# SBUF start addresses of matmul operands in a hybrid attention and convolution layer: pools in another order, small constants in one filled-up tile

## The chip, the cores and the metric

The kernel runs on one core of a Trainium2 chip. The metric is the device time of one execution in microseconds; the time before is the median of three executions.

## What is computed

One layer over 1024 positions of 1024 features, all in float32. The reference, cut to what matters:

```python
h = rms_norm(x, pre_norm_gain)
q, k, v, z_a, b_gate, c_gate, u, z_c = jnp.split(h @ w_in, 8, axis=-1)
attn = diff_attention(q, k, v, lam, slopes)        # 4 heads, two softmax maps each, chunk-causal
attn = rms_norm(attn, subln_gain, 1e-5) * 0.8 * silu(z_a)
conv_out = b_gate * conv3(c_gate * u) * silu(z_c)
mixed = jnp.concatenate([attn, conv_out], axis=-1) @ w_out
x = x + rms_norm(mixed, post_norm_gain)
e = rms_norm(p @ w_ple_proj, ple_norm_gain)
out = x + jax.nn.sigmoid(x @ w_ple_gate) * e
```

## The kernel before

Features lie on the 128 partitions, positions along the free dimension; the 1024 positions are two halves of 512 columns, and 1024 features are eight tiles of 128 (`kt`). Every float32 product is made of three matmuls in the 4-byte float32r type: `split` (L81 to L87) writes a value as a high and a low part, and `mm3` (L93 to L96) issues high x high (L94), high x low (L95) and low x high (L96) into one PSUM bank. The first operand, `lhsT`, is the stationary one, 128 columns loaded before each matmul; the second, `rhs`, streams through, 512 columns as a rule.

The stages, in order of time:

- the layer embedding (`embed`, tile `ple`), which starts while the inputs still arrive;
- the input projections (`product`, L122 to L126, tile `pj`): weight tiles `w` are stationary, the normalised input `hT` streams; each product of one weight tile with one half is 24 matmuls;
- the values (`v`): here slices of `hT` are stationary and the weights `wv` stream;
- per head, scores (L232, tile `s`, `qs` stationary, `ks` streaming), softmax, transposes of the probabilities (L259, tile `tpw`), and the product with the values (tile `av`, `vs` stationary, `wt` streaming), with the convolution's projections (`pj` again) laid between them by the table `PLAN`;
- the output projection (`out_half`, tile `o<-mT`), its norm (`post`, L529 to L537), and the gate (`gate_half`, L541 to L559, tile `o<-x`), which for each tile and half loads `e` from DRAM (L546), scales it (L547), waits for the product's tanh (L556), finishes `e` (L557, L558) and stores it (L559). `e` has three buffers.

The tiles `mT` and `x` of the last stage use the buffers of `hT`. The order of instructions on each engine comes from a scheduler that simulates the program; transfers all go through the SyncE queue.

SBUF space is given out in the order in which pools are opened and tiles are taken from them, each tile at the next multiple of 32 bytes. Before, pool `const` comes first (L49) and holds, beside two 512-byte matrices, five tiles of 16 to 148 bytes; everything after it starts at an odd multiple of 32. Start addresses, in bytes modulo 512, of what the matmuls read:

| matmuls | streaming operand | starts at | stationary operand | starts at | count |
|---|---|---|---|---|---|
| `pj`, `o` | hT, mT, x | 32 | w | 192 | 2136 |
| `v` | wv | 288 | hT | 32 | 192 |
| `ple`, `s`, `av` | pth, ks, wt | 288 | wph, qs, vs | 288 | 432 |
| `tpw` | ident | 128 | p0 to p3 | 288 | 144 |

Of the kernel before, what the change touches and what calls it, by code (L numbers as in the profile page):

```python
# [12 lines left out]
F32 = mybir.dt.float32  # L13
# [7 lines left out]
P = 128  # L21
S = 1024
D = 1024
NT = S // P
KT = D // P
HALF = 512
# [17 lines left out]
def hybrid_layer(ctx, tc, xT, pT, w_in, small, lams, w_out, w_ple, w_gate, outT):  # L44
    nc = tc.nc
    V, A, T, G = nc.vector, nc.scalar, nc.tensor, nc.gpsimd
    mult, add, sub = ALU.mult, ALU.add, ALU.subtract

    const = ctx.enter_context(tc.tile_pool(name="const", bufs=1))  # L49
    dram = ctx.enter_context(tc.tile_pool(name="dram", bufs=1, space=DRAM))  # L50
    hp = ctx.enter_context(tc.tile_pool(name="hp", bufs=16))
    mixp = ctx.enter_context(tc.tile_pool(name="mixp", bufs=1))
    tiny = ctx.enter_context(tc.tile_pool(name="tiny", bufs=3))
    rawp = ctx.enter_context(tc.tile_pool(name="rawp", bufs=3))
    wp = ctx.enter_context(tc.tile_pool(name="wp", bufs=3))
    ps_s = ctx.enter_context(tc.tile_pool(name="ps_s", bufs=3, space=PSUM))
    ps_a = ctx.enter_context(tc.tile_pool(name="ps_a", bufs=1, space=PSUM))

    def bank_s(name):
        return ps_s.tile([P, HALF], F32, tag="s", bufs=3, name=name)  # L60
# [7 lines left out]
    ident = const.tile([P, P], F32, name="ident")  # L68
    make_identity(nc, ident)
    fold = const.tile([P, P], F32, name="fold")  # L70
    own = const.tile([P, 4], F32, name="own")
    nhalf = const.tile([P, 16], F32, name="nhalf")
    G.memset(nhalf, -0.5)
    sm = const.tile([P, 37], F32, name="sm")
    subg = const.tile([P, 1], F32, name="subg")
    rs_e = const.tile([P, 32], F32, name="rs_e")

    def col(base, k):
        return sm[:, base + k:base + k + 1]
# [9 lines left out]
    def rsqrt(out, ssq, n, eps):  # L89
        V.tensor_scalar(out=out, in0=ssq, scalar1=1.0 / n, scalar2=eps, op0=mult, op1=add)  # L90
        G.tensor_tensor(out=out, in0=out, in1=nhalf[:, :ssq.shape[-1]], op=ALU.pow)
# [7 lines left out]
    def column_sums(acc, pool, extra=None, tag="flip"):  # L99
        flip = pool.tile([P, HALF], F32, tag=tag, name="flip")  # L100
        V.transpose(out=flip, in_=acc)
        part = tiny.tile([P, 32], F32, tag="part", name="part")
        V.tensor_reduce(out=part[:, 0:16], in_=flip.rearrange("p (f r) -> p f r", r=32), axis=AX.X, op=add)
        if extra is not None:
            V.tensor_tensor(out=part[:, 16:32].rearrange("p (t f) -> p t f", t=4),
                            in0=extra.unsqueeze(2).broadcast_to([P, 4, 4]),
                            in1=own.unsqueeze(1).broadcast_to([P, 4, 4]), op=mult)
        n = 16 if extra is None else 32
        ms = bank_t("ms")
        T.matmul(out=ms[:, :n], lhsT=fold, rhs=part[:, :n], start=True, stop=True)  # L110
        return ms
# [30 lines left out]

    hT = operand("hT")
    mix = [[mixp.tile([P, HALF], F32, tag="mix", bufs=16, name=f"mix{k}_{n}") for n in range(2)] for k in range(KT)]
    gt = mixp.tile([P, HALF + 2], F32, name="gt")
    R = [const.tile([P, HALF], F32, name=f"R{n}") for n in range(2)]

    with ExitStack() as st:
        qk = st.enter_context(tc.tile_pool(name="qk", bufs=1))
        rowp = st.enter_context(tc.tile_pool(name="rowp", bufs=3))  # L150

        lam_in = gt[:, 0:256].rearrange("p (a b) -> p a b", a=4)
        lam_e = qk.tile([P, 2], F32, name="lam_e")
        nlam = qk.tile([P, 1], F32, name="nlam")

        def mixing_weight():
            nc.sync.dma_start(out=lam_in.rearrange("p a b -> p (a b)"), in_=lams.partition_broadcast(P))
# [11 lines left out]
        class Head:  # L169
# [45 lines left out]
            def softmax(s, i):  # L215
                ii = i % 4
                W = (i + 1) * P
                qi = slice(i * P, i * P + P)
                nm = tiny.tile([P, 4], F32, tag="nm", name="nm")
                l = tiny.tile([P, 2], F32, tag="l", name="l")  # L220
                first = min(W, HALF) if W - HALF >= 256 or W <= HALF else W - 256
                chunks = [(0, first), (first, W - first)][:1 if W <= HALF else 2]
                low = [3.0e38] * 2
                pr = [ap.tile([P, S], F32, tag=f"p{ii}", name=f"p{ii}"), a2.tile([P, S], F32, tag="p1", name="p1")]
                for ci, (c0, n) in enumerate(chunks):
                    nn = max(256, n)
                    c = slice(c0, c0 + nn)
                    b0 = S - W + c0
                    banks = [bank_s(f"s{m}") for m in range(2)]
                    for m in range(2):  # L230
                        for part in range(2):
                            T.matmul(out=banks[m][:, :nn], lhsT=s.qs[:, m, qi], rhs=s.ks[:, m, part, c],  # L232
                                     start=part == 0, stop=part == 1)
                    for m in range(2):
                        new = nm[:, 2 * m + ci:2 * m + ci + 1]
                        V.tensor_tensor_reduce(out=pr[m][:, c0:c0 + n], in0=banks[m][:, :n], in1=s.bias[:, b0:b0 + n],  # L236
                                               scale=-1.0, scalar=low[m], op0=add, op1=ALU.min, accum_out=new)
                        low[m] = new
                for m in range(2):
                    A.activation(out=pr[m][:, :W], in_=pr[m][:, :W], func=AF.Exp, scale=-1.0, bias=low[m],  # L240
                                 accum_out=l[:, m:m + 1])
                if ii == 0:
                    s.r0 = tiny.tile([P, 4], F32, tag="r0", name="r0")
                rl = tiny.tile([P, 1], F32, tag="rl", name="rl")
                V.reciprocal(out=s.r0[:, ii:ii + 1], in_=l[:, 0:1])
                V.reciprocal(out=rl, in_=l[:, 1:2])
                V.scalar_tensor_tensor(out=rl, in0=rl, scalar=l[:, 0:1], in1=nlam, op0=mult, op1=mult)
                V.scalar_tensor_tensor(out=pr[0][:, :W], in0=pr[1][:, :W], scalar=rl, in1=pr[0][:, :W], op0=mult, op1=add)
                s.ws[ii] = pr[0]
# [98 lines left out]
        with ExitStack() as st0:  # L348
            vp = st0.enter_context(tc.tile_pool(name="vp", bufs=1, reuse_waits="tile"))
            v2 = st0.enter_context(tc.tile_pool(name="v2", bufs=2, reuse_waits="tile"))  # L350
            r_col = qk.tile([P, NT], F32, name="r_col")

            def sums_x(n):
                acc = R[n]
                A.activation(out=acc, in_=mix[0][n], func=AF.Square)
                for kt in range(1, KT):
                    sq = rowp.tile([P, HALF], F32, tag="t", name="sqx")
                    A.activation(out=sq, in_=mix[kt][n], func=AF.Square)
                    V.tensor_tensor(out=acc, in0=acc, in1=sq, op=add)
                return acc  # L360

            def row_scale(n):
                r = tiny.tile([P, 16], F32, tag="rs", name="rsx")
                rsqrt(r, column_sums(sums_x(n), rowp, tag="t")[:, :16], D, 1e-6)
                spread(R[n], r)
                for g in range(4):
                    A.copy(out=r_col[32 * g:32 * g + 32, 4 * n:4 * n + 4], in_=r[32 * g:32 * g + 32, g:16:4])

            head0 = Head(0)
            row_scale(0)  # L370
            row_scale(1)
            run([(wq, head0.ev_q), (wk, head0.ev_k)], (0,))
            run([(wq, head0.ev_q), (wk, head0.ev_k)], (1,), bank_s)
            run([(w_in_tile(3, 0, V), head0.ev_z)])
            wv = vp.tile([P, 2, KT, HALF], F32R, name="wv")
            for h in range(H):
                raw = rawp.tile([P, KT, P], F32, tag="raw", name="raw")
                nc.sync.dma_start(out=raw, in_=w_in[8 + h])
                c = slice(h * P, (h + 1) * P)
                split(wv[:, 0, :, c], wv[:, 1, :, c], raw)  # L380
            for j in range(NT):
                c = slice(j % 4 * P, j % 4 * P + P)
                ps = bank_p("v")
                for kt in range(KT):
                    b = hT[j // 4][kt]
                    mm3(ps, b[:, 0, c], b[:, 1, c], wv[:, 0, kt], wv[:, 1, kt], kt == 0, kt == KT - 1)
                v = v2.tile([P, 2, HALF], F32R, tag="v", name="v")
                split(v[:, 0], v[:, 1], ps, r_col[:, j:j + 1])
                nc.sync.dma_start(out=v_dram[j], in_=v.bitcast(F32))
        ap = st.enter_context(tc.tile_pool(name="ap", bufs=1, reuse_waits="tile"))  # L390
        a2 = st.enter_context(tc.tile_pool(name="a2", bufs=2, reuse_waits="tile"))
# [224 lines left out]
```

## Time and profile before

| | before |
|---|---|
| median of 3 runs | 660.55 us (659.13 to 661.38) |
| the profiled execution: its own time | 659.43 us |
| the profiled execution: span, first to last instruction | 657.7 us |
| PE busy | 644.0 us (98%), 2941 matmuls |
| DVE busy | 447.0 us (68%) |
| ACT, POOL busy | 243.2 us (37%), 229.3 us (35%) |
| DMA, mean over the span | 67.77 MB, 103 GB/s |
| mean granted TensorE clock | 0.996 of full |

The duration that the profile gives to a matmul is modelled and holds the way through the array too, so that durations overlap. How fast matmuls follow each other is read from their start times.

### The profile page before, as it was taken

The page shows a single profiled execution, that of the slowest core. Times are in us where ns is not written, and L with a number is a line of the kernel's source. Part 1 is how long each engine was busy: PE and PEld are TensorE (multiplying, and loading weights), DVE is VectorE, ACT ScalarE, POOL GpSimd, SP SyncE. Part 2 cuts the span into 40 slices and gives each one's busy share as a digit, 9 for nine tenths or more (in the row PEclk, how much of TensorE's full clock was granted, in tenths as well). Part 3 has the DMA queues.
Part 4 walks back from the last instruction along what each step waited for, and adds up shares of the span by engine and source line. Part 5 has one row for each costly group of instructions (what it writes and reads, how often), then busy time and mean ns, then how long its engine had stood idle before and what let it go on. Part 6 is the DMA issues. An engine that isn't in the chain of part 4 may idle for free.

```text
span 657.7 us, 8063 instructions
## 1 busy us (share of the span) xinstructions
PE 644.0 (98%) x2941; PEld 523.8 (80%) x2941; DVE 447.0 (68%) x821; ACT 243.2 (37%) x442; POOL 229.3 (35%) x114
## 2 busy tenths in 40 slices
PE   8899999999999999999999999999999999999994
PEld 4688888888888888888888888888888888888884
DVE  6968412698686687876886999439781199796233
ACT  7944312333462333543344434113631227131110
POOL 2016100325236534256362142424560278460000
PEclk9999999999999999999999999999999999999998
DMA  8966522210254112352012400103240025142222
GB/s 283 402 252 192 191 97 89 90 47 3 78 145 134 43 33 80 103 156 64 33 48 81 129 32 33 64 33 129 69 155 0 22 75 192 33 144 97 95 81 96
DMA packets 35654, 67.77 MB, mean 103 GB/s; under 512 B 3744, under 2 KB 12448, under 8 KB 35616
## 3 DMA queue, kind: packets, MB, share of 16 engines
q1 hardware_dynamic: 35616, 67.27, 31.3%
q8 instruction: 23, 0.38, 0.2%
q14 instruction: 15, 0.12, 0.1%
HBM read 48.38 MB, written 12.58 MB: 93 GB/s over the span
## 4 chain that ended last, share of the span: by engine, by line
PE 83%; DMA 8%; DVE 6%; issue 1%; ACT 1%; SPq 0%; DVEq 0%
PE pj L96 16%; PE pj L95 16%; PE pj L94 16%; PE s L232 5%; PE o L95 5%; PE o L96 5%; PE o L94 5%; DMA e<-e_dram 4%; DMA out_dram<-e 3%; PE tpw L259 2%; PE v L95 2%; PE v L96 2%; PE v L94 2%; DVE e L558 2%; PE av L96 1%; PE av L95 1%
## 5 line engine op out<-in xcount | busy, mean ns | idle before, releaser
L94 PE MATMUL pj<-hT,w 128*128 128x512 f32 x448 | 178.0, 398 | 1.1 <-ACT w L83 1.1
L95 PE MATMUL pj<-hT,w 128*128 128x512 f32 x448 | 178.5, 398 | 0.0
L96 PE MATMUL pj<-hT,w 128*128 128x512 f32 x448 | 177.9, 398 | 0.0
L84 POOL TENSOR_TENSOR w<-raw,w 128x1024 fp32r<-128x1024 f32 x41 | 106.5, 2608 | 146.0 <-ACT w L83 146.0
L94 PEld LDWEIGHTS pj<-hT,w 128*128 128x128 f32 x448 | 84.2, 188 | 20.2 <-ACT w L83 2.0
L96 PEld LDWEIGHTS pj<-hT,w 128*128 128x128 f32 x448 | 84.2, 188 | 18.2
L95 PEld LDWEIGHTS pj<-hT,w 128*128 128x128 f32 x448 | 84.2, 188 | 18.1
L240 ACT ACTIVATE p<-p,nm 128x128 f32<-128x128 f32 (+7 forms) x64 | 49.4, 772 | 67.5 <-DVE nm L236 57.6
L83 ACT CAST w<-raw 128x1024 fp32r<-128x1024 f32 x44 | 45.9, 1048 | 22.5 <-issue 13.4
L96 PE MATMUL o<-x,w 128*128 128x512 f32 (+1 forms) x136 | 52.4, 386 | 0.0
L95 PE MATMUL o<-x,w 128*128 128x512 f32 (+1 forms) x136 | 51.8, 381 | 0.0
L94 PE MATMUL o<-x,w 128*128 128x512 f32 (+1 forms) x136 | 51.6, 379 | 0.0
L95 PE MATMUL o<-mT,w 128*128 128x512 f32 x128 | 50.8, 397 | 0.0
L96 PE MATMUL o<-mT,w 128*128 128x512 f32 x128 | 50.5, 396 | 0.0
L94 PE MATMUL o<-mT,w 128*128 128x512 f32 x128 | 50.3, 393 | 0.0
L232 PE MATMUL s<-ks,qs 128*128 128x512 f32 (+2 forms) x192 | 47.8, 348 | 0.0
L84 DVE TENSOR_TENSOR wt<-tpw,wt 128x512 fp32r<-128x512 f32 (+3 forms) x48 | 25.2, 551 | 28.9 <-ACT wt L83 28.8
L83 ACT CAST wt<-tpw 128x512 fp32r<-128x512 f32 (+3 forms) x48 | 21.2, 479 | 63.3 <-PE tpw L259 63.2
L236 DVE CUSTOM_DVE_ANT_0 p<-s,bias 128x512 f32<-128x512 f32 (+3 forms) x64 | 34.9, 565 | 9.7 <-PE s L232 5.7
L547 DVE SCALAR_TENSOR_TENSOR e<-e,sm,re 128x512 f32<-128x512 f32 x16 | 16.3, 1017 | 36.7 <-DMA e<-e_dram 36.7
L401 POOL TENSOR_TENSOR mix<-mix,R 128x512 f32<-128x512 f32 x8 | 11.5, 1436 | 75.9 <-DVE mix L400 73.8
L232 PEld LDWEIGHTS s<-ks,qs 128*128 128x128 f32 x192 | 33.4, 188 | 5.3
(139 smaller groups left out, 1118.3 us busy)
## 6 DMA issues: line engine op xcount, KB each, us to landing
raw<-in_w_in SPq DMA_DIRECT2D x32, 512.0 KB, 3.5
mix<-in_xT SPq DMA_DIRECT2D x16, 256.0 KB, 6.1
e_dram<-e SPq DMA_DIRECT2D x16, 256.0 KB, 5.5
mix<-e_dram SPq DMA_DIRECT2D x16, 256.0 KB, 3.2
ks<-ks SPq DMA_DIRECT2D x16, 256.0 KB, 3.6
v_dram<-v SPq DMA_DIRECT2D x8, 512.0 KB, 2.6
vs<-v_dram SPq DMA_DIRECT2D x32, 128.0 KB, 2.8
raw<-in_w_out SPq DMA_DIRECT2D x8, 512.0 KB, 3.2
```

The costliest lines, as they stand in the source:

```text
L83: A.copy(out=hi, in_=src)
L84: (lo_eng or V).tensor_tensor(out=lo, in0=src, in1=hi.bitcast(F32), op=sub)
L94: T.matmul(out=ps, lhsT=ah, rhs=bh, start=first, stop=False)
L95: T.matmul(out=ps, lhsT=ah, rhs=bl, start=False, stop=False)
L96: T.matmul(out=ps, lhsT=al, rhs=bh, start=False, stop=last)
L232: T.matmul(out=banks[m][:, :nn], lhsT=s.qs[:, m, qi], rhs=s.ks[:, m, part, c], start=part == 0, stop=part == 1)
L236: V.tensor_tensor_reduce(out=pr[m][:, c0:c0 + n], in0=banks[m][:, :n], in1=s.bias[:, b0:b0 + n], scale=-1.0, scalar=low[m], op0=add, op1=A ...
L240: A.activation(out=pr[m][:, :W], in_=pr[m][:, :W], func=AF.Exp, scale=-1.0, bias=low[m], accum_out=l[:, m:m + 1])
L259: T.transpose(out=tp[:, ii * P:(ii + 1) * P], in_=s.ws[ii][:, j * P:(j + 1) * P], identity=ident)
L401: G.tensor_tensor(out=o, in0=o, in1=R[n], op=mult)
L547: V.scalar_tensor_tensor(out=e, in0=e, scalar=col(C_PLE, m), in1=re[n], op0=mult, op1=mult)
L558: V.tensor_tensor(out=e[:, c], in0=e[:, c], in1=mix[m][n][:, c], op=add)
```

## The change

The pools are opened in another order (`edge`, `hp`, `wp`, `rawp`, `mixp`, `const`, `tiny`), the small constants become slices of one tile of 384 bytes that fills the space up to address 1536, the odd-sized tiles `gt` and `r_col` (filled up to 352 bytes) stand behind the matmul operands, and `lam_e` and `nlam` leave the pool `qk`. `R`, which is no matmul operand, moves behind them. The probability tiles get the width that they need, 640, 768, 896 and 1024 columns in place of 1024 for all.

```diff
+    edge = ctx.enter_context(tc.tile_pool(name="edge", bufs=1))
+    hp = ctx.enter_context(tc.tile_pool(name="hp", bufs=16))
+    wp = ctx.enter_context(tc.tile_pool(name="wp", bufs=3))
+    rawp = ctx.enter_context(tc.tile_pool(name="rawp", bufs=3))
+    mixp = ctx.enter_context(tc.tile_pool(name="mixp", bufs=1))
     const = ctx.enter_context(tc.tile_pool(name="const", bufs=1))
+    tiny = ctx.enter_context(tc.tile_pool(name="tiny", bufs=3))
     dram = ctx.enter_context(tc.tile_pool(name="dram", bufs=1, space=DRAM))
-    hp = ctx.enter_context(tc.tile_pool(name="hp", bufs=16))
-    mixp = ctx.enter_context(tc.tile_pool(name="mixp", bufs=1))
-    tiny = ctx.enter_context(tc.tile_pool(name="tiny", bufs=3))
-    rawp = ctx.enter_context(tc.tile_pool(name="rawp", bufs=3))
-    wp = ctx.enter_context(tc.tile_pool(name="wp", bufs=3))
+
+    small_c = edge.tile([P, 96], F32, name="small_c")
...
-    own = const.tile([P, 4], F32, name="own")
-    nhalf = const.tile([P, 16], F32, name="nhalf")
+    own = small_c[:, 0:4]
+    nhalf = small_c[:, 4:20]
     G.memset(nhalf, -0.5)
-    sm = const.tile([P, 37], F32, name="sm")
-    subg = const.tile([P, 1], F32, name="subg")
-    rs_e = const.tile([P, 32], F32, name="rs_e")
+    sm = small_c[:, 20:57]
+    subg = small_c[:, 57:58]
+    rs_e = small_c[:, 58:90]
+    lam_e = small_c[:, 90:92]
+    nlam = small_c[:, 92:93]
...
-    gt = mixp.tile([P, HALF + 2], F32, name="gt")
+    gt = const.tile([P, HALF + 2], F32, name="gt")
+    r_col = const.tile([P, NT + 80], F32, name="r_col")[:, :NT]
...
-                pr = [ap.tile([P, S], F32, tag=f"p{ii}", name=f"p{ii}"), a2.tile([P, S], F32, tag="p1", name="p1")]
+                pr = [ap.tile([P, HALF + P * ii + P], F32, tag=f"p{ii}", name=f"p{ii}"), a2.tile([P, S], F32, tag="p1", name="p1")]
```

Every operand of the 2,904 matmuls in the table above now starts at a multiple of 512. The instructions are the same on all engines, and so is the order on SyncE's queue. The scheduler puts 123 of 2,927 matmuls, all of the last head and the beginning of the output projection, at other places, and some rows of DVE, ACT and POOL beside them.

PE, where the probabilities of the last head's second half begin to be transposed (`tpw`, between projections `pj` and value products `av`), before:

```order
L95 MATMUL av<-wt,vs 128x512
L96 MATMUL av<-wt,vs 128x512
L94 MATMUL av<-wt,vs 128x512
L95 MATMUL av<-wt,vs 128x512
L96 MATMUL av<-wt,vs 128x512
L259 MATMUL tpw<-ident,p_3457 128x128
L259 MATMUL tpw<-ident,p_3485 128x128
L259 MATMUL tpw<-ident,p_3512 128x128
L259 MATMUL tpw<-ident,p_3539 128x128
```

PE at the same place with the change:

```order
L100 MATMUL pj<-hT_6_108,w 128x512
L101 MATMUL pj<-hT_6_108,w 128x512
L101 MATMUL av<-wt,vs 128x512
L102 MATMUL av<-wt,vs 128x512
L100 MATMUL av<-wt,vs 128x512
L264 MATMUL tpw<-ident,p_3454 128x128
L264 MATMUL tpw<-ident,p_3482 128x128
L101 MATMUL av<-wt,vs 128x512
L102 MATMUL av<-wt,vs 128x512
L264 MATMUL tpw<-ident,p_3509 128x128
L264 MATMUL tpw<-ident,p_3536 128x128
```

The same matmuls stand there in another mix: projections come between the value products, and value products between the transposes.

DVE in the gate's loop (scale `e`, finish with tanh, add the residual `mix`), before:

```order
L547 SCALAR_TENSOR_TENSOR e<-e,sm,re_5045 128x512
L557 SCALAR_TENSOR_TENSOR e<-tg,e 128x512
L558 TENSOR_TENSOR e<-e,mix_0_121 128x512
L547 SCALAR_TENSOR_TENSOR e<-e,sm,re_5045 128x512
L557 SCALAR_TENSOR_TENSOR e<-tg,e 128x512
```

DVE at the same place with the change:

```order
L551 SCALAR_TENSOR_TENSOR e<-e,small_c,re_5042 128x512
L561 SCALAR_TENSOR_TENSOR e<-tg,e 128x512
L562 TENSOR_TENSOR e<-e,mix_0_120 128x512
L551 SCALAR_TENSOR_TENSOR e<-e,small_c,re_5042 128x512
L561 SCALAR_TENSOR_TENSOR e<-tg,e 128x512
```

Only the source of the column factors has another name; nothing moved in this loop.

## Rows read from the trace of the kernel before

**Rows 1.** The page: busy time by engine, granted TensorE clock in 40 slices.

```profile
PE 644.0 (98%) x2941; PEld 523.8 (80%) x2941; DVE 447.0 (68%) x821; ACT 243.2 (37%) x442; POOL 229.3 (35%) x114
...
PEclk9999999999999999999999999999999999999998
```

**Rows 2.** Stretches: start:end and length, busy us (x instructions) by engine, clock, DMA share, GB/s.

```profile
0.00:22.00 22.00, 17.83 (x64) 11.02 (x65) 16.77 (x35) 17.07 (x28) 4.44 (x9) 1.00 0.91 313
49.60:567.00 517.40, 517.40 (x2390) 424.49 (x2390) 361.40 (x688) 195.28 (x363) 207.46 (x97) 1.00 0.26 84
567.00:657.70 90.70, 81.86 (x376) 66.82 (x374) 47.41 (x65) 13.40 (x24) 15.03 (x8) 0.97 0.31 99
```

**Rows 3.** PE's waits: line waited for, us in total, times, longest.

```profile
PE idle L331 <- DVE zero L328: 1.2, 1, 1.2
PE pj L94 <- ACT w L83: 1.1, 2, 0.7
```

**Rows 4.** The chain that ended last: start us, us, what.

```profile
567.04 0.07 PE ms L110 x2
567.11 2.02 DMA out_dram<-e
569.14 2.77 DMA e<-e_dram
...
626.87 2.01 DMA out_dram<-e
628.89 2.45 DMA e<-e_dram
631.46 0.75 DVE e L547
632.22 0.61 DVE e L558
632.84 2.32 DMA out_dram<-e
```

**Rows 5.** Matmul groups from 49.6 to 567 us: count, busy us, mean ns (modelled).

```profile
L95 PE MATMUL pj<-hT,w 128*128 128x512 f32 x425 | 169.4, 399 | 0.0
...
L95 PE MATMUL o<-mT,w 128*128 128x512 f32 x128 | 50.8, 397 | 0.0
...
L232 PE MATMUL s<-ks,qs 128*128 128x512 f32 x80 | 25.6, 403 | 0.0
L94 PE MATMUL v<-wv,hT 128*128 128x512 f32 x64 | 24.9, 390 | 0.0
...
L95 PE MATMUL av<-wt,vs 128*128 128x512 f32 x24 | 9.5, 395 | 0.0
...
L95 PE MATMUL o<-x,w 128*128 128x512 f32 x12 | 4.7, 394 | 0.0
```

**Rows 6.** PE in order of time, output projection: start us, duration, what.

```profile
500.15 0.39 PE L96 MATMUL o<-mT,w 128*128 128x512 f32 x1
500.38 0.39 PE L94 MATMUL o<-mT,w 128*128 128x512 f32 x1
500.61 0.40 PE L95 MATMUL o<-mT,w 128*128 128x512 f32 x1
...
512.75 0.39 PE L96 MATMUL o<-mT,w 128*128 128x512 f32 x1
```

**Rows 7.** PE in order of time, values.

```profile
95.14 0.39 PE L96 MATMUL v<-wv,hT 128*128 128x512 f32 x1
...
109.42 0.39 PE L96 MATMUL v<-wv,hT 128*128 128x512 f32 x1
```

**Rows 8.** PE in order of time, gate in pieces of 256 columns.

```profile
643.18 0.28 PE L96 MATMUL o<-x,w 128*128 128x256 f32 x1
...
648.58 0.27 PE L96 MATMUL o<-x,w 128*128 128x256 f32 x1
```

**Rows 9.** Two stretches: output projection, busy softmax stage (columns as in rows 2).

```profile
500.00:514.00 14.00, 14.00 (x62) 11.27 (x61) 1.38 (x2) 2.30 (x5) 0.00 (x0) 1.00 0.00 1
...
300.00:400.00 100.00, 100.00 (x484) 82.83 (x483) 81.44 (x191) 40.43 (x80) 38.99 (x18) 1.00 0.22 66
```

**Rows 10.** PE in order of time, gate in full width.

```profile
578.31 0.40 PE L96 MATMUL o<-x,w 128*128 128x512 f32 x1
578.54 0.39 PE L94 MATMUL o<-x,w 128*128 128x512 f32 x1
578.77 0.39 PE L95 MATMUL o<-x,w 128*128 128x512 f32 x1
579.01 0.40 PE L96 MATMUL o<-x,w 128*128 128x512 f32 x1
```

More of the change, by code (lines that the diff above doesn't have):

```diff
@@ L152, in hybrid_layer @@
         lam_in = gt[:, 0:256].rearrange("p (a b) -> p a b", a=4)
-        lam_e = qk.tile([P, 2], F32, name="lam_e")
-        nlam = qk.tile([P, 1], F32, name="nlam")
         def mixing_weight():
@@ L350, in hybrid_layer @@
             v2 = st0.enter_context(tc.tile_pool(name="v2", bufs=2, reuse_waits="tile"))
-            r_col = qk.tile([P, NT], F32, name="r_col")
             def sums_x(n):
```

## Prediction

> **What bounds the kernel now.** I read the page first: PE is busy 98% of the span, every other engine at most 68%, and the granted clock is full in all slices but the last [rows 1], which is the upper of its two levels, 2.4 GHz. A busy PE is not yet a PE at its peak, so the stretches come next. From 49.6 to 567 us PE is busy for 517.40 of 517.40 us [rows 2], and the list of PE's waits has six rows, the longest wait being 1.2 us, all in the first 24 us [rows 3]. So in that stretch nothing makes PE wait: its length is the number of matmuls times the pace at which they follow each other.
>
> The chain of waits corrects this for the end. Its last PE piece is the small matmul of the second half's norm at 567.04 us; behind it stand only transfers and DVE work to the end at 657.7 us [rows 4]. In the gate's loop a store of `e` (2.01 us), the load into the freed buffer (2.45 us), the scaling (0.75 us) and the residual of an older tile (0.61 us) follow each other, some 6.0 us for one tile and half with the small steps between [rows 4], while its 24 matmuls take 24 x 0.233 = 5.6 us. PE ends at 648.9 us [rows 8], some 9 us ahead of the span. A faster PE buys nothing behind 567 us.
>
> Now the pace, from start times. In the output projection 54 matmuls start between 500.15 and 512.75 us, 12.60 / 54 = 233.3 ns each [rows 6]; 512 columns at 2.4 GHz are 213.3 ns, so 20 ns of each are not columns. Other engines do not cause it: in that stretch the DMA share is 0.00 and DVE is busy for 1.38 of 14 us [rows 9]. In the values stage, with the same type and shape and at the same clock, 63 matmuls take from 95.14 to 109.42 us, 14.28 / 63 = 226.7 ns [rows 7]. What differs are the operands: which tile is stationary, and where they start, 288 and 32 against 32 and 192 modulo 512. Matmuls of 256 columns take 5.40 / 45 = 120.0 ns [rows 8], 13.3 ns over their 106.7 ns of columns. So there is a surplus of 6 to 12%, and some of it changes with the operands.
>
> **The change part by part.**
>
> *Start addresses.* No instruction is added or taken away, so the only possible gain is the pace. Ahead of 567 us stand, by line, 425 + 425 + 423 matmuls of `pj`, 3 x 128 of `o<-mT` and 12 + 12 + 11 of `o<-x` [rows 5] (one of the three lines of each group stands there), 1,692 in all at the slower pace. No row shows operands at multiples of 512, so the price is bounded by what is near. Upper bound of the gain: the whole surplus goes, 20.0 ns x 1,692 = 33.8 us, 13.3 ns x 192 `v` = 2.6 us, and 20 ns for 80 `s` and 72 `av` of full width, if they run at the pace of `pj`, 3.0 us; 39.4 us together. Lower bound: nothing, or a loss, since aligning all operands also makes all of them alike (see the last rival). I take the nearest row, the pace of `v`, the fastest that this kernel shows for this shape: 1,692 x 6.67 ns = 11.3 us. I leave out the 72 `pj` ahead of 49.6 us, where transfers hold 0.91 of the DMA engines in the first 22 us [rows 2] and a faster PE would wait for `x`, and `s` and `av` (at most 152 x 6.67 ns = 1.0 us).
>
> *The tail.* 90.7 us from 567 us on, with its 376 matmuls [rows 2], nothing: the DVE loop and SyncE's order in it are unchanged, and the round of transfers sets it. If the surplus went there too, PE would only end more than 9 us ahead.
>
> *Another order in the last head.* 123 matmuls change places in a stretch in which PE now waits for nothing [rows 2]. Nothing to gain; if a transposed tile then came late, the cost would be about the longest wait that PE shows, 1.2 us [rows 3]. I take zero: projections stand between the value products in both versions.
>
> *One tile for the constants.* The danger would be false waits between users of different slices. The writers are few and early, and DVE, which does most of the reading, executes in order. I take zero; the same 1.2 us bounds it.
>
> *Narrower probability tiles, moved `R`, `gt`, `r_col`.* No instruction changes its size: zero.
>
> *Other limits.* At 11.3 us less in 517 us, 2%, the busiest stretch of DVE goes from 81.44 of 100 us [rows 9] to 83%: no new bound. If the whole surplus went, it would be some 88%, and a few softmax steps could come late; that is the cover that the upper bound needs.
>
> The sum is made against the profiled execution's own 659.4 us, which is 1.1 us under the median of the three runs: 659.4 - 11.3 = 648.1 us. I forecast **648 us**; its own range is 641 to 655 us, since operands at 512 may save a little more or only half of that step.
>
> **The rivals.**
>
> *The whole surplus goes.* The surplus would be the price of operands that do not start on a boundary, in the values stage too. For it: the streaming operand starts at 32 past a multiple of 256 in both stages, so neither row shows an aligned one, and both have a surplus. Against it: it would be the largest possible effect, and 13.3 ns of surplus at 256 columns, where the stretch read less [rows 8], look at least in part like a price for each matmul, such as exchanging the stationary operand, which stays. Time: 659.4 - 39.4 = 620 us. The Trainium skill, TensorE: Matmul & The Clock Gate, section "Wait — 56ns, not 53.3ns?", gives 215.7 ns from start to start for 512 columns at the full clock, measured in bf16. No run here shows it; by that figure the same counts would save 29.8 + 2.1 + 2.7 us, and the estimate would be 625 us.
>
> *Addresses do not matter.* The 6.67 ns between the stages would come from the roles of the tiles: in the values stage the stationary parts lie 2 KB apart and the streaming ones 16 KB, in the projections 4 KB and 2 KB, and the change leaves these distances. The change then does not do what it is meant to: 660 us. For it: every tile already starts at a multiple of 32 bytes and every operand is read in sequence. The Trainium skill, SBUF — State Buffer, section "Door 1", says that SBUF is read in lines of 16 bytes and that consecutive accesses to one line run at full rate; by that rule these operands are on a line's start before and after, and the time stays. The trace does not contradict it, but shows a surplus that the rule leaves unexplained.
>
> *Equal starts collide.* PE streams one operand while it loads the next stationary one. After the change both start at the same residue, 0. If the two reads then met in the same part of the memory, each matmul would be held. For it: `s` and `av`, which have equal residues (288 and 288) now, have means of 403 and 395 ns in the modelled durations, `v`, whose residues lie 256 apart, 390 [rows 5]. Against it: `av` is no slower than `pj` (399). In the gate one of three matmuls takes 0.24 us and the two others 0.23 [rows 10]; if all took 0.240 us, it would cost 6.7 ns x 1,692 = 11.3 us and the time would be 671 us. This decides from a mean pace of about 234.5 ns on, where the loss passes 2 us, 0.3% of the time.
>
> **How the numbers follow.** The forecast has 0.36: it asks only for a pace that the trace already shows. That the whole surplus goes has 0.27, no effect of addresses 0.21, the collision 0.16. Within 0.3% of 660.55 us, 2 us, is about what cannot be told from no change. So faster is 0.36 + 0.27 = 0.63, the same 0.21, slower 0.16. The range leaves out the collision and the last of the largest gain: 620 us, the upper bound, to 661 us, the unchanged time with half a microsecond of spread.
>
> **What the profile of the changed kernel would show.** Right: starts in the output projection 226 to 227 ns apart, as those of the values; the `ms` matmul of the second half at about 556 us instead of 567.04; some 90 us behind it with the same round of store, load and scaling; PE's waits as few as now. Between 213 and 217 ns apart says the first rival, 233 the second, 235 or more the third. I am wrong in the tail if the stretch behind the last `ms` shrinks with the matmuls. I am wrong on the order or the constants if PE shows new waits on DVE between 400 and 490 us, or if the time changes while the pace does not.

## The result and the profile after

The median of four executions after is 652.2 us (651.04 to 653.69); four of the kernel before on the same chip have 659.98 us. The ratio is 0.9875 (0.9853 to 0.9898): faster by 1.25%, 7.8 us. The profiled execution takes 651.04 us with a span of 649.3 us, 8.4 us less than before in both.

The page after, busy time and granted clock, answering to [rows 1]:

```profile
PE 631.8 (97%) x2941; PEld 523.2 (81%) x2941; DVE 447.8 (69%) x821; ACT 243.7 (38%) x442; POOL 227.0 (35%) x114
...
PEclk9999999999999999999999999999999999999997
```

Two stretches after, cut at the `ms` matmul of the second half as in [rows 2]:

```profile
49.60:557.70 508.10, 507.87 (x2388) 423.83 (x2388) 360.94 (x687) 195.71 (x363) 206.16 (x97) 1.00 0.27 85
557.70:649.30 91.60, 79.81 (x376) 66.91 (x374) 48.58 (x66) 13.40 (x24) 13.94 (x9) 0.96 0.30 98
```

The first stretch is 9.3 us shorter with the same work; the second is 0.9 us longer. PE waits hardly more than before: its list of waits has seven rows where it had six [rows 3], the longest still 1.2 us. The first of them, and the only new one, for DVE at the second half's norm:

```profile
PE ple L100 <- ACT pth L89: 1.2, 1, 1.2
...
PE ms L116 <- DVE part L109: 0.2, 1, 0.2
```

The pace in the output projection after, PE in order of time; the two rows stand 54 matmuls apart, as in [rows 6]:

```profile
500.32 0.39 PE L102 MATMUL o<-mT,w 128*128 128x512 f32 x1
...
512.56 0.39 PE L102 MATMUL o<-mT,w 128*128 128x512 f32 x1
```

12.24 / 54 = 226.7 ns instead of 233.3. The values, whose operands moved from 32 and 288 to 0 and 0, keep their pace; the two rows stand 63 matmuls apart, as in [rows 7]:

```profile
89.79 0.39 PE L102 MATMUL v<-wv,hT 128*128 128x512 f32 x1
...
104.07 0.39 PE L102 MATMUL v<-wv,hT 128*128 128x512 f32 x1
```

14.28 / 63 = 226.7 ns again. Not every projection runs so fast. PE in order of time after, where transposes interrupt it:

```profile
177.72 0.93 PE L264 MATMUL tpw<-ident,p 128*128 128x128 f32 x7
...
178.71 0.39 PE L100 MATMUL pj<-hT,w 128*128 128x512 f32 x1
...
180.10 0.39 PE L100 MATMUL pj<-hT,w 128*128 128x512 f32 x1
```

Six matmuls from 178.71 to 180.10 us take 231.7 ns each. After such a piece it takes from one to ten matmuls of 512 columns, six by the median, until the starts are 226.7 ns apart; ahead of that, but for the first step, they vary mostly between 224 and 236 ns.

The chain that ended last, after, from the second half's norm on, answering to [rows 4]:

```profile
556.04 0.69 DVE part L109
556.73 1.59 DVE e L561
558.34 0.69 DVE e L562
559.03 0.03 DVE rso L96
559.06 1.98 DMA out_dram<-e
561.05 2.69 DMA e<-e_dram
...
629.67 0.75 DVE e L551
630.42 0.61 DVE e L562
631.06 2.02 DMA out_dram<-e
```

The first store of this round starts at 559.06 us instead of 567.11, and the round of store, load, scaling and residual is the same. What stands behind that store took 657.7 - 567.11 = 90.6 us before and takes 649.3 - 559.06 = 90.2 us now.

### The profile page after: what moved, and what is told of

Its sections match the earlier page's. It is cut to its first block, busy times and chain, and to the rows that moved or that the text cites. A ratio compares the mean times of both kernels' runs of the same rounds, so it can differ in the third digit from the quotient of the medians.

```text
span 649.3 us, 8064 instructions
## 1 busy us (share of the span) xinstructions
PE 631.8 (97%) x2941; PEld 523.2 (81%) x2941; DVE 447.8 (69%) x821; ACT 243.7 (38%) x442; POOL 227.0 (35%) x114
## 4 chain that ended last, share of the span: by engine, by line
PE 71%; DVE 12%; DMA 9%; ACT 3%; issue 2%; POOL 2%; DVEq 0%; POOLq 0%; ACTq 0%
PE pj L100 14%; PE pj L102 14%; PE pj L101 14%; PE s L237 5%; DMA e<-e_dram 4%; DMA out_dram<-e 3%; DVE mix L539 3%; PE o L102 3%; PE o L100 3%; PE o L101 3%; PE tpw L264 2%; PE v L100 2%; PE v L101 2%; PE v L102 2%; DVE x L90 2%
## 5 line engine op out<-in xcount | busy, mean ns | idle before, releaser
L100 PE MATMUL pj<-hT,w 128*128 128x512 f32 x448 | 176.4, 394 | 1.2 <-ACT w L89 1.2
L101 PE MATMUL pj<-hT,w 128*128 128x512 f32 x448 | 176.2, 393 | 0.0
L102 PE MATMUL pj<-hT,w 128*128 128x512 f32 x448 | 176.1, 393 | 0.0
L102 PE MATMUL o<-x,w 128*128 128x512 f32 (+1 forms) x136 | 51.3, 377 | 0.0
L100 PE MATMUL o<-x,w 128*128 128x512 f32 (+1 forms) x136 | 51.2, 377 | 0.0
L101 PE MATMUL o<-x,w 128*128 128x512 f32 (+1 forms) x136 | 51.2, 377 | 0.0
L100 PE MATMUL o<-mT,w 128*128 128x512 f32 x128 | 49.8, 389 | 0.0
L101 PE MATMUL o<-mT,w 128*128 128x512 f32 x128 | 49.8, 389 | 0.0
L102 PE MATMUL o<-mT,w 128*128 128x512 f32 x128 | 49.7, 390 | 0.0
L551 DVE SCALAR_TENSOR_TENSOR e<-e,small_c,re 128x512 f32<-128x512 f32 x16 | 16.3, 1017 | 36.5 <-DMA e<-e_dram 36.5
```

Of the source, the lines that this page charges most:

```text
L100: T.matmul(out=ps, lhsT=ah, rhs=bh, start=first, stop=False)
L101: T.matmul(out=ps, lhsT=ah, rhs=bl, start=False, stop=False)
L102: T.matmul(out=ps, lhsT=al, rhs=bh, start=False, stop=last)
L551: V.scalar_tensor_tensor(out=e, in0=e, scalar=col(C_PLE, m), in1=re[n], op0=mult, op1=mult)
```

## The experiments

Theories. *Difference*: the pace depends on how far apart the starts of the streaming and the stationary operand lie. *Streaming*: only the streaming operand's start counts. *Stationary*: only the stationary operand's. *Multiples of 512*: each start must be one. Where no single rows are shown, the pace is told as the time from the first matmul of one `kt` to that of the next, three matmuls: 680 ns is 226.7 each, 700 ns is 233.3. A difference is always stationary start minus streaming start.

**Streaming operand of the projections at 32, all else at 0** (e2_h32). An unused tile behind `hp` keeps the rest in place.

```diff
     hp = ctx.enter_context(tc.tile_pool(name="hp", bufs=16))
+    fa = ctx.enter_context(tc.tile_pool(name="fa", bufs=1))
...
-    small_c = edge.tile([P, 96], F32, name="small_c")
+    small_c = edge.tile([P, 104], F32, name="small_c")
+    fa_t = fa.tile([P, 120], F32, name="fa_t")
```

> The changed kernel with the other thing put back: hT, mT and x start at 32 modulo 512 again, everything else at 0. Stationary theory: 227 ns in the projections, 652 us; in the values stage hT at 32 is the stationary operand, as it was before, when it ran at 227 ns. Streaming theory: 233 ns in projections, output projection and gate, about 660 us. Difference theory: 233 ns in the projections, and the values, where the difference is 32 too, slow down as well.

Measured: 660.92 us against 661.79 before, ratio 0.9996 (0.998 to 1.0012). The same 54 matmuls of its output projection, PE in order of time:

```profile
500.04 0.40 PE L102 MATMUL o<-mT,w 128*128 128x512 f32 x1
...
512.64 0.40 PE L102 MATMUL o<-mT,w 128*128 128x512 f32 x1
```

12.60 / 54 = 233.3 ns: 32 bytes undo the whole gain, with the order, the constants' tile and the narrower tiles still in place. The values, where `hT` is stationary at 32 and `wv` streams from 0, fall to 14.70 / 63 = 233.3 ns as well, by the rows

```profile
95.10 0.40 PE L103 MATMUL v<-wv,hT 128*128 128x512 f32 x1
...
109.80 0.40 PE L103 MATMUL v<-wv,hT 128*128 128x512 f32 x1
```

*Streaming* had no place for that, and *Stationary* none for the slower projections. The run also strikes out the rival of the prediction that the tiles' roles and distances, not their addresses, made the difference.

**Stationary operand of the projections at 192, all else at 0** (e1_w192).

```diff
+    fa = ctx.enter_context(tc.tile_pool(name="fa", bufs=1))
     wp = ctx.enter_context(tc.tile_pool(name="wp", bufs=3))
+    fb = ctx.enter_context(tc.tile_pool(name="fb", bufs=1))
...
+    fa_t = fa.tile([P, 48], F32, name="fa_t")
+    fb_t = fb.tile([P, 80], F32, name="fb_t")
```

> The changed kernel with one thing put back: the three weight buffers of the projections start at 192 modulo 512 again (a filler of 192 bytes before them, 320 behind), everything else stays at 0. Five of the eight weight tiles of the output projection and of the gate lie in another pool and stay at 0, so both starts can be compared inside one run. Stationary theory (the start of the stationary operand sets the surplus): products with weights at 192 take 233 ns for each matmul, those with weights at 0 227 ns, and the time returns by about 6 to 8 us, to 658 us or more. Streaming theory (the start of the streaming operand does): 227 ns in both, 652 us. Difference theory (the distance between the two starts modulo 512 does): 233 ns too, so only the next run tells it from the stationary theory.

Measured: 654.47 us, ratio 0.9893 (0.9875 to 0.9911). Some weights stand in buffers of other pools, at 0, so that both cases are in one run. PE in order of time, 12 matmuls with `w` at 192 and then 21 with `w` at 0:

```profile
533.36 0.39 PE L106 MATMUL o<-mT,w 128*128 128x512 f32 x1
...
536.10 0.39 PE L106 MATMUL o<-mT,w 128*128 128x512 f32 x1
...
537.01 0.39 PE L104 MATMUL o<-mT,w 128*128 128x512 f32 x1
...
541.77 0.39 PE L104 MATMUL o<-mT,w 128*128 128x512 f32 x1
```

2.74 / 12 = 228.3 ns (687 / 3 = 229 by the medians) and 4.76 / 21 = 226.7. The stationary operand counts too, but 192 costs a third of the step, not all of it. No theory had foretold that: *Stationary* and *Difference* both asked for 233 ns here. So it is not a matter of off or on a boundary; the size of the difference enters.

**All at 32** (e6_all32: `small_c` with 104 columns) **and the streaming operand at 256, all else at 0** (e7_h256: 160 columns and a filler of 256 bytes behind `hp`).

> The changed kernel with all pools behind the constants moved by 32 bytes: every matmul operand starts at 32 modulo 512, none at a multiple of 512. Difference theory: 680 ns for a triple in all stages, as in the changed kernel, and the same time, 652 us. Boundary theory (a start on a multiple of 512 is what counts): 700 ns and about 660 us.

> The changed kernel with hT, mT and x at 256 modulo 512 and everything else at 0. In the sweep of streaming starts the times of a triple repeated after 256 bytes, and before the change the values ran at 680 ns with starts of 288 and 32. Difference theory with a period of 256: 680 ns in all stages, 652 us. If the starts must be equal modulo 512: 690 ns or more in projections, output projection and gate, 656 us or more.

Measured: 652.51 us, ratio 0.9876 (0.9851 to 0.9901), and 651.6 us, ratio 0.9858 (0.9837 to 0.9879). Output projection of the first, 54 matmuls:

```profile
500.17 0.39 PE L100 MATMUL o<-mT,w 128*128 128x512 f32 x1
...
512.41 0.39 PE L100 MATMUL o<-mT,w 128*128 128x512 f32 x1
```

and of the second:

```profile
499.81 0.39 PE L103 MATMUL o<-mT,w 128*128 128x512 f32 x1
...
512.05 0.39 PE L103 MATMUL o<-mT,w 128*128 128x512 f32 x1
```

Both 12.24 / 54 = 226.7 ns. *Multiples of 512* falls: the same 32 bytes that cost everything in one operand cost nothing in both, and starts that are equal modulo 256 are enough.

**Differences in steps of 32** (one execution each, 662.98, 661.09 and 658.24 us). e5_w8 gives eight weight tiles the starts 0, 32, ... 224 and adds two probes at its end; e3_hsweep makes the tiles of `hp` 4128 bytes wide, so that the streaming start moves by 32 with each `kt`; e4_wsweep pads each block of weights by 32 bytes.

```diff
# e5_w8
+        w = (pool or wp).tile([P, 2 * KT * P + 8], F32R, tag="w", name="w")[:, :2 * KT * P].rearrange("p (a k c) -> p a k c", a=2, k=KT)
# e3_hsweep
+        return [[hp.tile([P, 2 * HALF + 8], F32R, tag="H", name=f"{name}{n}_{kt}")[:, :2 * HALF].rearrange("p (a b) -> p a b", a=2)
# e4_wsweep
+        w = (pool or wp).tile([P, 2, KT, P + 8], F32R, tag="w", name="w")[:, :, :, :P]
```

> The changed kernel with the eight weight buffers at eight starts: three at 160, 192 and 224 modulo 512 (all of the projections, three tiles of each later stage), five at 0, 32, 64, 96 and 128; everything else at 0. Every product of 24 matmuls then has one distance between its two starts, and can settle to its own pace. Behind the last product stand 30 matmuls with a stationary operand of 128 columns and 30 with one of 32, all at 0, whose results nobody reads. Difference theory: 0 settles at 680 ns for a triple and 192 at 687, as in the run with weights at 192; 224 is the distance that streaming at 32 had, 699 to 700; 160 is that of the kernel with streaming at 32 and weights at 192, turned, about 700; 32, 64, 96 and 128 each have their own value between 680 and 706. Streaming theory: 680 everywhere. The probes: if the 13.3 ns that are left at 680 come from the load of the next stationary operand, which reads while the matmul streams, the 32-column probe runs at 217 to 220 ns, the 128-column one at 227; if they belong to each matmul, both run at 227.

> The sixteen buffers of hT, mT and x get a pitch of 4128 bytes, so that they start at the sixteen multiples of 32 modulo 512; all other operands stay at 0. In the output projection and the gate each triple of matmuls then streams from another start. Streaming theory: most starts take 700 ns for a triple, a few (0, perhaps 128, 256, 384, if a coarser line than 512 counts) 680 ns. Stationary theory: 680 ns for all. Difference theory: a table that depends on the start, with a mean between 680 and 700 ns. If some start is faster than 680 ns, the surplus of 13.3 ns that is left is one of addresses too.

> Each block of 128 weight columns gets a pitch of 544 bytes, so that the stationary operands of one weight tile start at sixteen multiples of 32 modulo 512 (32 x kt for the high part, 256 + 32 x kt for the low part); the streaming operands stay at 0. Stationary theory: the time of a triple depends on kt, 680 ns only where both starts are favourable. Streaming theory: 680 ns for every kt. Difference theory: a table by kt, in line with the one of the streaming sweep when the sign is turned.

In e5_w8 each whole product of the output projection has one difference. PE in order of time, 12 matmuls with `w` at 0 and 12 with `w` at 32:

```profile
513.41 0.39 PE L105 MATMUL o<-mT,w 128*128 128x512 f32 x1
...
516.13 0.39 PE L105 MATMUL o<-mT,w 128*128 128x512 f32 x1
...
546.76 0.40 PE L104 MATMUL o<-mT,w 128*128 128x512 f32 x1
...
549.56 0.40 PE L104 MATMUL o<-mT,w 128*128 128x512 f32 x1
```

2.72 / 12 = 226.7 and 2.80 / 12 = 233.3 ns. Settled, with the streaming operand at 0, the mean:

| stationary start | 0 | 32 | 64 | 96 | 128 | 160 | 192 | 224 |
|---|---|---|---|---|---|---|---|---|
| ns for three matmuls | 680 | 700 | 700 | 702 | 697 | 700 | 687 | 700 |

The table agrees with the runs that have these differences elsewhere: before, 192 - 32 = 160 (700); e1_w192, 192 (687); e2_h32, 0 - 32 = 224 modulo 256 (700) and in its values 32 (700); the values of before, 32 - 288 = 0 modulo 256 (680). Where the difference changes with every third matmul, nothing settles: in e3_hsweep the median of no start comes below 693 ns, not even that of 0, and the eight figures for 0 to 224 return for 256 to 480; in e4_wsweep they lie between 686 and 704. The two sweeps were expected to agree and do not: a difference of 96 takes 705 ns in the first and 688 in the second. So behind a change the pace depends on more than a matmul's own difference, and on what is open. A stationary operand of 32 columns, tried in e5_w8 at equal starts to make its load short (109 ns instead of 188), ran at some 232 ns, where 217 to 220 or 227 were expected; so the surplus was not shown to be the length of that load.

Matmuls of 256 columns do not follow the table. In the gate's pieces they take 120.0 ns at a difference of 160 [rows 8] and also at 0, in the kernel after. At 224, in e2_h32, they take 5.30 / 45 = 117.8 ns, and at 192, in e1_w192, as little:

```profile
644.21 0.28 PE L104 MATMUL o<-x,w 128*128 128x256 f32 x1
...
649.51 0.28 PE L104 MATMUL o<-x,w 128*128 128x256 f32 x1
```

So equal starts are the fast case of the 512 columns, not of every width.

**Other operands behind the end** (e10_probes, one execution): the kernel after with six buffers for `e` (below) and, at its end, five groups of 24 matmuls of 512 columns that nothing reads; its time of 667.98 us contains them.

```diff
+        for probe in range(5):
+            for k in range(24):
+                i, j = k % 16, (k + 5) % 16
+                if probe == 0:
+                    l, r = hv[i][:, 0, :P], hv[j][:, k % 2]
+                elif probe == 1:
+                    l, r = hv[3][:, 0, :P], hv[j][:, k % 2]
+                elif probe == 2:
+                    l, r = h16[:, (k % 4) * P:(k % 4 + 1) * P], h16[:, (k % 2) * HALF:(k % 2 + 1) * HALF]
+                elif probe == 3:
+                    l, r = h16[:, (k % 4) * P:(k % 4 + 1) * P], h16[:, (k % 2) * HALF + 16:(k % 2 + 1) * HALF + 16]
+                else:
+                    l, r = hv[i][:, 0, 8:8 + P], hv[j][:, k % 2]
```

> The changed kernel with six buffers for e, and behind its last product five times 24 matmuls of 512 columns whose results nobody reads: float32r with equal starts and a new stationary operand each time; float32r with the same stationary operand each time; bf16 with equal starts; bf16 streaming from 32 and stationary from 0; float32r streaming from 0 and stationary from 32. Read theory (both operands are read from SBUF at the same time and hold each other up, and 4-byte columns leave no slack): 227, 227, 214 to 217, 214 to 217 and 233 to 234 ns. If the 13.3 ns that are left belong to any matmul with a new stationary operand, bf16 shows 227 too, and the repeated operand less than 227. If starts matter for 2-byte columns, the fourth group is slower than the third.

PE in order of time: the first group's settled part (18 matmuls), then the two bf16 groups (45 matmuls):

```profile
639.00 0.39 PE L602 MATMUL probe<-x,x 128*128 128x512 f32 x1
...
643.08 0.62 PE L602 MATMUL probe<-x,x 128*128 128x512 f32 x2
...
648.75 0.39 PE L602 MATMUL probe<-h 128*128 128x512 bf16 x1
...
658.47 0.59 PE L602 MATMUL probe<-h 128*128 128x512 bf16 x2
```

float32r at equal starts: 4.08 / 18 = 226.7 ns, and the same with one stationary operand for the whole group. That operand was loaded anew for each matmul all the same (24 loads of 188 ns in the trace), so the group does not show what a matmul without a load would take. bf16: 9.72 / 45 = 216.0 ns, whether the starts are equal or 32 bytes apart; its loads took 98 ns. The last group, float32r with the stationary start at 32, took 233 ns.

**More buffers for `e`**, in the kernel after (e8_e6bufs) and in the one before (e9_before_e6).

```diff
-            e = c4.tile([P, HALF], F32, tag="e", bufs=3, name="e")
+            e = c4.tile([P, HALF], F32, tag="e", bufs=6, name="e")
```

> The changed kernel with six buffers for e in the gate's loop in place of three. Tail theory (the round of store, load and scaling sets the end, PE is some 9 us ahead): the loads run ahead, the round no longer closes, the end follows PE by some 4 to 5 us, and the time falls by 5 to 8 us to about 645 us. If the transfers themselves were the limit, or DVE were, the time stays at 652 us.

> The kernel before, with its old starts, and six buffers for e in place of three. Tail theory: with the old pace PE ends at about 649 us of the span and the end follows 4 to 5 us later, so about 655 us, 0.992 of before. The distance to the changed kernel with six buffers, 643.8 us, is then what the starts alone are worth where nothing else binds, 11 us, the 11.3 us that the pace promised ahead of 567 us plus 2 us of the gate, less what narrow matmuls take back. If the pace had other causes than the starts, or the six buffers helped by something else, the distance would stay near 8 us.

Measured: 643.78 us, ratio to before 0.9738 (0.9716 to 0.9761), and 655.48 us, 0.9907 (0.9881 to 0.9933). The chain of e8_e6bufs in order of time, at its end:

```profile
637.82 0.13 PE o L102
637.97 0.39 ACT tg L560
638.38 0.44 DVE e L561
638.85 0.42 DVE e L562
```

and that of e9_before_e6:

```profile
648.77 0.13 PE o L96
648.92 0.39 ACT tg L556
649.34 0.44 DVE e L557
649.80 0.42 DVE e L558
```

In both the round of transfers has gone from the chain and PE's last matmul sets the end. Three buffers cost 661.57 - 655.48 = 6.1 us before, and 652.2 - 643.8 = 8.4 us after the change, where 5 to 8 were expected. With PE bound to the end, the start addresses are worth 655.48 - 643.78 = 11.7 us, between two chips whose kernels before take 661.57 and 661.68 us; 11 were expected. e8_e6bufs beats both kernels.

## Why the prediction was right, and where its sum was off

*What bounds.* Right in the main. PE's matmuls at their pace set the time first, the round of transfers sets it last, and e8_e6bufs, in which only that round was relieved, shows the second half of this. Missing was a passage between the two that belongs to DVE (below).

*Start addresses: 226.7 ns.* The pace was right, to the 0.1 ns, and this was partly luck: the values' pace was taken because it was the nearest row, with no reason why operands on multiples of 512 should have it. The reason, equal starts modulo 256 in both cases, came only from the experiments. The term was too large, 11.3 us for 9.2. From starts, `ms` of the second half came 566.88 - 557.68 = 9.2 us earlier. By kind, as sums of start-to-start times of the same matmuls: `o<-mT` 2.54 us (2.56 asked), `o<-x` 0.23 (0.23), but the 1,273 `pj` 300.5 - 294.9 = 5.6 us where 1,273 x 6.67 ns = 8.5 us were asked. Those projections are laid between transposes, scores and narrow value products, and after each such piece they start 224 to 236 ns apart before they settle. Without the steps of more than 245 ns (48 before, 47 after) their mean fell from 233.2 to 228.3 ns, not to 226.7. The sum took a pace from a stage of equal matmuls and used it for a mixed one. What was left out, `s`, `av`, `tpw` and `ms` (0.7 us together) and all ahead of 49.6 us (0.1 us), gives the rest of 9.2.

*The tail.* Nothing asked, 0.4 us found in one execution of each: PE now ends its matmuls 11.4 us earlier, and as foretold this bought nothing.

*What no step named.* 1.1 of the 9.2 us were lost at the passage into the tail. DVE in order of time before, at the second half's norm (`rso` comes behind `ms`, 566.88 us):

```profile
565.14 1.21 DVE L557 SCALAR_TENSOR_TENSOR e<-tg,e 128x512 f32<-128x512 f32 x1 [0.40 <-ACT tg L556]
566.39 0.69 DVE L558 TENSOR_TENSOR e<-e,mix 128x512 f32<-128x512 f32 x1
567.20 0.18 DVE L90 TENSOR_SCALAR rso<-ms 128x16 f32<-128x16 f32 x1
```

and after (`ms` at 557.68 us):

```profile
556.64 1.67 DVE L561 SCALAR_TENSOR_TENSOR e<-tg,e 128x512 f32<-128x512 f32 x1
558.34 0.69 DVE L562 TENSOR_TENSOR e<-e,mix 128x512 f32<-128x512 f32 x1
558.95 0.17 DVE L96 TENSOR_SCALAR rso<-ms 128x16 f32<-128x16 f32 x1
```

Before, `rso` started 0.32 us behind the start of `ms`; now it stands 1.27 us behind it, since DVE still has two passes over `e` in front. The first store does not wait for `ms`, as the chain in [rows 4] lets one think, but for the second of these passes: it starts 0.03 us behind the pass's end at 567.08 and at 559.03 us. DVE comes to that pass through a stretch of almost unbroken work that begins at the first half's norm, before at 526.43 and after at 518.43 us (columns as in [rows 2], the third busy time is DVE's):

```profile
526.43:567.11 40.68, 40.68 (x178) 32.74 (x177) 38.93 (x29) 17.84 (x28) 31.31 (x15) 1.00 0.31 105
518.43:559.06 40.63, 40.63 (x181) 33.65 (x181) 40.08 (x30) 17.89 (x28) 30.91 (x15) 1.00 0.33 107
```

DVE is busy for 96% of this stretch before and 99% after, and the stretch is as long as it was, although PE gains another 1.2 us in it. The prediction looked for DVE's limit in the softmax stage alone, 81.44 of 100 us. Why DVE's passes in the stretch took 1.15 us more in sum is not shown. PE came earlier by 9.2 us, `rso` by 567.20 - 558.95 = 8.25, the first store by 8.05. With the 0.4 us of the tail that is the 8.4 us of the spans: 652.2 us against the 648 forecast.

*Order, constants, narrower tiles: zero.* Right: PE's one new wait is 0.2 us, and e2_h32, which keeps all of them, is back at the time before.

*The rivals.* The whole surplus did not go: 226.7 ns, not 213 to 217. That addresses do not matter is refuted by e2_h32. Equal starts do not collide; the opposite holds, equal starts are the good case. The modelled durations of `s` and `av` that spoke for it say nothing of their pace, and the one matmul of three at 0.24 us in [rows 10] is rounding: three take 700 ns. The values had equal starts modulo 256 already, and that is why they were faster, though the prediction counted them as a case with different ones.

## What to carry to other kernels

Give the streaming and the stationary tile of float32r matmuls of 512 columns the same start modulo 256 bytes; multiples of 512 are only one way to it. For another width, time it first: here 256 columns were 2.2 ns faster at differences of 192 and 224 than at equal starts. Read the pace from start to start, apart for stages of equal matmuls and for mixed ones, since a busy share near 100% hides a surplus and a mixed stage spends much of its time unsettled. Before counting a gain at the end of the kernel, look whether another engine or another round sets the way there: here three more buffers gave another 8.4 us and let the rest of the gain through.

## What the runs showed of the hardware

Shown: for float32r the pace of 512 columns at the upper clock level is 226.7 ns where the difference of the two starts is 0 modulo 256 bytes, and 229 to 234 ns at the seven other multiples of 32; behind other matmuls it takes up to ten to settle. 256 columns take 120.0 ns at differences of 0 and 160 and 117.8 at 192 and 224. Argued only: that the load of the next stationary operand and the streaming reads hold each other up in SBUF. By the Trainium skill, TensorE: Matmul & The Clock Gate, section "Step-by-step: what each phase is for", loading the next weights takes no read bandwidth from the running matmul; here a move of one operand alone, e2_h32, cost 6.7 ns a matmul. The rule does not account for that, but no run separates the two reads, so none shows it wrong.

Open: what holds the matmuls up, why 256 columns have another table than 512, and the 13.3 ns that 226.7 still lies over the 213.3 of the columns. bf16 has 216.0 in the same place, and the 215.7 ns that the same page gives for bf16, section "Wait — 56ns, not 53.3ns?", agree with it. Neither a repeated stationary operand, still loaded each time, nor a narrow one brought float32r nearer; no run goes further.
